# The second layer norm of a two-layer decoder trunk, re-divided between VectorE and ScalarE with GpSimd left out

## The chip, the cores and the metric

One core of a Trainium2 chip runs the whole kernel in one launch. The metric is the device time of one execution, in microseconds (us). The engines are called by the profile's short names: PE is TensorE, DVE is VectorE, ACT is ScalarE, POOL is GpSimd, SP is SyncE; SP only issues transfers here. Each engine takes its instructions strictly in the order in which the program put them on that engine's queue.

## What is computed

The program is a decoder trunk of two layers over 512 positions of 1024 features. Each layer mixes the positions, adds the residual and normalises (the first norm), then runs a mixture of experts, adds the residual and normalises again (the second norm). The second norm is what is changed:

```python
DN_ALPHA = (2.0 * DEPTH) ** 0.25
LN_EPS = 1e-5

def layer_norm(x, g, b):
    xf = x.astype(F32)
    mu = jnp.mean(xf, axis=-1, keepdims=True)
    var = jnp.mean(jnp.square(xf - mu), axis=-1, keepdims=True)
    return ((xf - mu) * lax.rsqrt(var + LN_EPS) * g.astype(F32) + b.astype(F32)).astype(x.dtype)

for layer in range(DEPTH):
    ...
    x = layer_norm(DN_ALPHA * x + mix.astype(x.dtype), ln1_g[layer], ln1_b[layer])
    ffn = hier_moe(x, ...)
    x = layer_norm(DN_ALPHA * x + ffn, ln2_g[layer], ln2_b[layer])
return x
```

## The kernel before

All products are made from float32 values split in two halves, `hi` (ACT, L195) and `lo` (DVE, L196), with three matmuls each (L200, L201, L202). The method `hilo` emits such a split; `mm3` emits the three matmuls.

The method `moe` runs the experts. Sixteen regular tiles and some overflow tiles are computed; each tile's rows are added into a DRAM tensor `yd` by a scatter that POOL issues (L1617). `yd` has been filled beforehand with the scaled residual. When the last scatter has landed, SP loads the four blocks of 128 positions back into four tiles `row`, 128 partitions by 1024 features (L1752). These are blocks 0 to 3; the second norm turns each `row` into the layer's output in place, and then `finish(tt, r)` is called.

What `finish` is differs by layer. In layer 0 it is `odd_token`: SP writes the block to the DRAM tensor `x2d` (L1291), PE transposes it in eight pieces (L209), ACT and DVE split the transposed block (L195, L196), and PE multiplies it with the value weights of the next layer's attention (24 matmuls). After block 3 PE goes on with the keys of the attention (tile `sd`), which need all four blocks. In layer 1 `finish` is one transfer to the output by SP (L1824), and block 3's transfer is the end of the program.

The norm before has these parts, each on one block `tt` or on a pair of blocks:

- `stats` (L1764): two DVE BN_STATS over 512 features (L290) and one aggregate (L1766), giving mean and variance.
- `scale` (L1770): for two blocks at once, the reciprocal root of the variance in eleven tiny DVE instructions that wait for one another (`rsqrt_steps`, L271 to L281), and a twelfth (L1773) that gives minus mean times scale.
- `norm` (L1776): the upper 512 features go through ACT (L1778), then POOL for the product with `g` (L1779), then the addition of `b`, by POOL for blocks 0 and 1 (L1781) and by DVE for blocks 2 and 3 (L1787). The lower 512 features take two DVE passes (L1782, L1784).

The generators are interleaved by `weave`, which alternates between a main generator and a side one. So the order on DVE is written out by hand: statistics of blocks 0 and 1; statistics of 2 and 3 woven with the first `scale`; norms of 0 and 1 woven with the second `scale`; norms of 2 and 3:

```python
run_all(each(stats, 0, 1))
weave(each(stats, 2, 3), scale(0))
weave(each(norm, 0, 1), scale(1))
run_all(each(norm, 2, 3))
```

`moe` calls `lnparams` for the tiles `g` and `b` (names `lng`, `lnb`) long before. The four tiles `self.xg` are the buffers of gathered rows, which no instruction reads any more by the time of the norm.

Of the kernel before, what the change touches and what calls it, by code (L numbers as in the profile page):

```python
# [8 lines left out]
F32 = mybir.dt.float32  # L9
# [4 lines left out]
AF = mybir.ActivationFunctionType  # L14
# [4 lines left out]
MUL, ADD, SUB = ALU.mult, ALU.add, ALU.subtract  # L19

L = 512
D = 1024
KD = D // 128
NT = L // 128
# [28 lines left out]
def blk(i, n=128):  # L53
    return slice(i * n, (i + 1) * n)


def weave(main, *sides):


    wait = [0] * len(sides)  # L60
    done = [False] * len(sides)

    def poke(i):
        while wait[i] <= 0 and not done[i]:
            try:
                wait[i] = next(sides[i])
            except StopIteration:
                done[i] = True
    for _ in main:
        for i in range(len(sides)):  # L70
            wait[i] -= 1
            poke(i)
    for i in range(len(sides)):
        for _ in (sides[i] if not done[i] else ()):
            pass


def run_all(gen):
    for _ in gen:
        pass  # L80
# [82 lines left out]
class Trunk:  # L163
# [99 lines left out]
        q.dma_start(bt, b.rearrange("(o d) -> o d", o=1).to_broadcast([128, D]))  # L263
        self.lnp = gt, bt

    def rsqrt_steps(self, z, var, n, pool, eps=1e-5):

        V = self.nc.vector
        t = lambda nm, dt=F32: pool.tile([128, n], dt, name="rq" + nm, bufs=4)
        h, m, y = t("h"), t("m"), t("i", I32)  # L270
        V.tensor_scalar(h, var, eps, 0.5, op0=ADD, op1=MUL)  # L271
        yield 1
        V.tensor_scalar(y, h.bitcast(I32), -0.5, float(0x5f3759df - 0x400000 - 0x80000000), op0=MUL, op1=ADD)
        y = y.bitcast(F32)
        for i in range(3):
            yield 1
            V.tensor_mul(m, y, y)
            yield 1
            V.tensor_mul(m, m, h)
            yield 1  # L280
            V.scalar_tensor_tensor(z, m, -1.5, y, op0=ADD, op1=MUL)  # L281
            y = z
# [1353 lines left out]
    def moe(self, layer, lg, between, start, before, after, finish):  # L1636
        nc, tc, mo, I = self.nc, self.tc, self.mo, self.I
# [110 lines left out]
        rows = []  # L1748
        mv = mo.tile([128, NT, 2], F32, name="bnmv4", bufs=1)
        for tt in range(NT):  # L1750
            r = mo.tile([128, D], F32, name="row", bufs=6)
# [1 line left out]
            rows.append(r)  # L1753
        after()
        V = nc.vector
        rs = mo.tile([128, NT], F32, name="lnrs", bufs=1)
        nm = mo.tile([128, NT], F32, name="lnnm", bufs=1)
        g, b = self.lnp
        lo, hi = blk(0, 512), blk(1, 512)
        sts = [mo.tile([128, 2, 6], F32, name="bnst", bufs=4) for _ in range(NT)]  # L1760

        def stats(tt):
            for h in range(2):
                self.ln_stats(sts[tt], rows[tt], h)  # L1764
                yield 1
            V.bn_aggr(mv[:, tt, :], sts[tt])  # L1766
            yield 1

        def scale(q):
            s = blk(q, 2)  # L1770
            yield from self.rsqrt_steps(rs[:, s], mv[:, s, 1], 2, mo)
            yield 1
            V.scalar_tensor_tensor(nm[:, s], mv[:, s, 0], -1.0, rs[:, s], op0=MUL, op1=MUL)  # L1773
            yield 1

        def norm(tt):  # L1776
            r = rows[tt]
            nc.scalar.activation(r[:, hi], r[:, hi], AF.Identity, scale=rs[:, tt:tt + 1], bias=nm[:, tt:tt + 1])  # L1778
            nc.gpsimd.tensor_mul(r[:, hi], r[:, hi], g[:, hi])  # L1779
            if tt < 2:  # L1780
                nc.gpsimd.tensor_add(r[:, hi], r[:, hi], b[:, hi])  # L1781
            V.scalar_tensor_tensor(r[:, lo], r[:, lo], mv[:, tt, 0:1], g[:, lo], op0=SUB, op1=MUL)  # L1782
            yield 1
            V.scalar_tensor_tensor(r[:, lo], r[:, lo], rs[:, tt:tt + 1], b[:, lo], op0=MUL, op1=ADD)  # L1784
            yield 1
            if tt >= 2:
                V.tensor_add(r[:, hi], r[:, hi], b[:, hi])  # L1787
            finish(tt, r)
            yield 1

        def each(f, *i):
            for j in i:
                yield from f(j)
        run_all(each(stats, 0, 1))
        weave(each(stats, 2, 3), scale(0))
        weave(each(norm, 0, 1), scale(1))
        run_all(each(norm, 2, 3))

    def run(self):
        nc, tc, I = self.nc, self.tc, self.I  # L1800
# [58 lines left out]
```

## Time and profile before

| what | us |
|---|---|
| median of three runs | 1006.04 |
| lowest and highest of them | 1003.46, 1008.68 |
| the profiled execution, its own time | 1003.56 |
| its span in the profile | 1001.9 |
| PE busy | 845.2 |
| DVE busy | 789.1 |
| ACT busy | 566.4 |
| POOL busy | 311.9 |

All positions in the rows below are microseconds from the start of that span; the execution's own time is 1.7 us longer. The second norm stands in the profile twice: in layer 0 from 535.97 us, when its first block has landed, and in layer 1 from 975.21 us to the end. The page's busy shares are means over the whole span and say little of these two places; they are read from the timeline of each engine in them.

### The profile page before, as it was taken

The page shows a single profiled execution, that of the slowest core. Times are in us where ns is not written, and L with a number is a line of the kernel's source. Part 1 is how long each engine was busy: PE and PEld are TensorE (multiplying, and loading weights), DVE is VectorE, ACT ScalarE, POOL GpSimd, SP SyncE. Part 2 cuts the span into 40 slices and gives each one's busy share as a digit, 9 for nine tenths or more (in the row PEclk, how much of TensorE's full clock was granted, in tenths as well). Part 3 has the DMA queues.
Part 4 walks back from the last instruction along what each step waited for, and adds up shares of the span by engine and source line. Part 5 has one row for each costly group of instructions (what it writes and reads, how often), then busy time and mean ns, then how long its engine had stood idle before and what let it go on. Part 6 is the DMA issues. An engine that isn't in the chain of part 4 may idle for free.

```text
span 1001.9 us, 13169 instructions
## 1 busy us (share of the span) xinstructions
PE 845.2 (84%) x4396; PEld 707.5 (71%) x4396; DVE 789.1 (79%) x1542; ACT 566.4 (57%) x922; POOL 311.9 (31%) x342
## 2 busy tenths in 40 slices
PE   5996999998975899999782899999993889999840
PEld 4895887787864788887661787788883668888630
DVE  6998668668679799997776657888788879999737
ACT  3331445536124899988673256656611688999721
POOL 6397971101102223222222302345611122232203
PEclk9998999999987999999995999989997799999975
DMA  9321112102947789999955350420093879999722
GB/s 280 123 93 43 43 43 95 43 1 61 358 174 260 296 299 365 371 375 305 322 177 191 105 127 1 120 50 2 4 365 140 327 251 337 361 382 362 239 65 114
DMA packets 52875, 192.05 MB, mean 192 GB/s; under 512 B 13492, under 2 KB 15552, under 8 KB 38336
## 3 DMA queue, kind: packets, MB, share of 16 engines
q1 hardware_dynamic: 37344, 156.47, 42.5%
q0 software_dynamic: 13440, 24.17, 9.2%
q10 hardware_dynamic: 2016, 10.49, 2.7%
q8 instruction: 38, 0.62, 0.2%
q14 instruction: 37, 0.30, 0.1%
HBM read 183.20 MB, written 31.98 MB: 215 GB/s over the span
## 4 chain that ended last, share of the span: by engine, by line
PE 47%; issue 15%; DVE 14%; DMA 12%; ACT 5%; POOL 5%; another core or an unknown queue 1%; ACTq 0%; SPq 0%; POOLq 0%; DVEq 0%
PE acc L200 10%; PE acc L202 10%; PE acc L201 10%; DMA yd<-row,r 8%; PE tp L209 2%; DVE u L196 2%; POOL yd L1617 2%; ACT u L195 1%; DMA xg<-x1d,r 1%; PE tp L1410 1%; POOL xg L1574 1%; DMA row<-yd 1%; PE sd L201 1%; PE sd L200 1%; POOL row L1779 1%
## 5 line engine op out<-in xcount | busy, mean ns | idle before, releaser
L200 PE MATMUL acc<-u 128*128 128x512 f32 (+1 forms) x712 | 296.5, 416 | 6.9 <-ACT u L195 6.9
L202 PE MATMUL acc<-u 128*128 128x512 f32 (+1 forms) x712 | 282.6, 397 | 5.5 <-DVE u L196 5.4
L201 PE MATMUL acc<-u 128*128 128x512 f32 (+1 forms) x712 | 281.7, 396 | 3.4 <-POOL u L196 1.9
L196 DVE TENSOR_TENSOR u<-u 128x1024 fp32r<-128x1024 f32 x142 | 172.2, 1241 | 27.0 <-ACT u L195 25.9
L195 ACT CAST u<-u 128x1024 fp32r<-128x1024 f32 x150 | 152.9, 1051 | 41.4 <-PE acc L202 36.6
L196 DVE TENSOR_TENSOR u<-rx,u 128x1024 fp32r<-128x1024 f32 x128 | 152.3, 1220 | 28.9 <-ACT u L195 27.8
L202 PEld LDWEIGHTS acc<-u 128*128 128x128 f32 x712 | 141.5, 199 | 35.6 <-DVE u L196 8.4
L200 PEld LDWEIGHTS acc<-u 128*128 128x128 f32 x712 | 143.8, 202 | 29.9 <-ACT u L195 8.7
L201 PEld LDWEIGHTS acc<-u 128*128 128x128 f32 x712 | 142.7, 200 | 25.8 <-DVE u L196 3.4
L1617 POOL DMA_INDIRECT yd<-row,r x37 | 58.8, 1588 | 239.1 <-ACT row L1616 186.8
L195 ACT CAST u<-rx 128x1024 fp32r<-128x1024 f32 x128 | 129.3, 1049 | 3.0 <-issue 1.8
L195 ACT CAST u<-tp 128x512 fp32r<-128x512 f32 x102 | 60.4, 608 | 72.0 <-PE tp L209 68.1
L196 DVE TENSOR_TENSOR u<-tp,u 128x512 fp32r<-128x512 f32 x102 | 67.8, 698 | 16.7 <-ACT u L195 16.6
L1574 POOL DMA_INDIRECT xg<-x1d,r x41 | 46.6, 1137 | 76.3 <-PE tp L209 66.2
L209 PE MATMUL tp<-idf,xg 128*128 128x128 f32 x312 | 49.9, 301 | 16.0 <-DMA xg<-x1d,r 9.8
L1400 POOL TENSOR_SCALAR P<-P,st 128x256 f32<-128x256 f32 (+3 forms) x32 | 35.1, 1097 | 90.3 <-DVE st L1376 55.2
L209 PEld LDWEIGHTS tp<-idf,xg 128*128 128x128 f32 x312 | 47.2, 208 | 21.3 <-issue 10.1
L200 PE MATMUL acc<-u,ht 128*128 128x512 f32 x148 | 58.5, 395 | 4.0 <-ACT ht L195 4.0
L202 PE MATMUL acc<-u,ht 128*128 128x512 f32 x148 | 57.7, 390 | 0.0
L201 PE MATMUL acc<-u,ht 128*128 128x512 f32 x148 | 57.6, 389 | 0.0
L1616 ACT ACTIVATE row<-acc,r 128x512 f32<-128x512 f32 x74 | 47.8, 687 | 10.0 <-PE acc L202 10.0
L1118 ACT COPY u<-tp 128x512 f32<-128x512 f32 x16 | 9.4, 587 | 66.3 <-PE tp L1117 56.3
(394 smaller groups left out, 1439.4 us busy)
## 6 DMA issues: line engine op xcount, KB each, us to landing
rx<-in_moe_w_gate_up_dram SPq DMA_DIRECT2D x48, 1024.0 KB, 10.8
u<-in_moe_w_gate_up_dram SPq DMA_DIRECT2D x24, 1024.0 KB, 16.2
u<-in_moe_w_down_dram SPq DMA_DIRECT2D x19, 1024.0 KB, 14.9
rx<-in_moe_w_down_dram SPq DMA_DIRECT2D x16, 1024.0 KB, 11.9
u<-in_ev_w_in_dram SPq DMA_DIRECT2D x10, 1024.0 KB, 6.2
u<-in_ev_w_out_dram SPq DMA_DIRECT2D x4, 1024.0 KB, 5.1
x1d<-row POOLq DMA_DIRECT2D x8, 512.0 KB, 5.6
yd<-row ACTq DMA_DIRECT2D x8, 512.0 KB, 3.6
```

The costliest lines, as they stand in the source:

```text
L195: self.nc.scalar.copy(hi, src)
L196: (self.nc.gpsimd if pool else self.nc.vector).tensor_sub(lo, src, hi)
L200: nc.tensor.matmul(ps, ah, bh, start=start, stop=False)
L201: nc.tensor.matmul(ps, ah, bl, start=False, stop=False)
L202: nc.tensor.matmul(ps, al, bh, start=False, stop=stop)
L209: self.nc.tensor.transpose(tp[:, blk(j)], src[:, s], self.idf)
L1400: nc.gpsimd.tensor_scalar(P[:, 1, :W], P[:, 1, :W], st[:, 5, 1:2], None, op0=MUL)
L1410: nc.tensor.transpose(tp[:, blk(2 * b + x)], P[:, x, blk(b0 + b)], self.idf)
L1574: nc.gpsimd.indirect_dma_start(out=xg, out_offset=None, in_=self.x1d, in_offset=bass.IndirectOffsetOnAxis(ap=self.toki[:, s:s + 1], axis=0 ...
L1616: nc.scalar.activation(ys[:, blk(c, 512)], yp[c], AF.Copy, scale=self.gate[:, s:s + 1])
L1617: return lambda: self.scattered(s, nc.gpsimd.indirect_dma_start(out=self.yd, out_offset=bass.IndirectOffsetOnAxis(ap=self.toki[:, s:s + 1] ...
L1779: nc.gpsimd.tensor_mul(r[:, hi], r[:, hi], g[:, hi])
```

## The change

It does six things.

1. POOL gets no work in the second norm. Both halves of a block are normalised by DVE at full width, in two passes of 128 by 1024: (row minus mean) times `g`, then times the scale plus `b`.
2. The statistics of blocks 2 and 3 move from DVE to ACT: one full pass `sums` gives the sum of a row, one pass `squares` gives the sum of the squared differences from the mean. Both use ACT's accumulator output; their full-size output goes into `xg` and is read by nobody. A DVE instruction `means` lies between them.
3. `rsqrt_steps` can take a sum of squares and divide by 1024 itself.
4. The twelfth instruction of `scale` (minus mean times scale) is gone.
5. In layer 0 the blocks come one by one: block 0 gets statistics, scale and norm before block 1's statistics.
6. In layer 1 blocks 0 and 1 keep a common `scale`; block 1 is normalised in halves, with the eleven instructions of the scale of blocks 2 and 3 put in threes between its four passes.

The diff, whole:

```diff
--- before.py
+++ after.py
@@ -263,12 +263,15 @@
         q.dma_start(bt, b.rearrange("(o d) -> o d", o=1).to_broadcast([128, D]))
         self.lnp = gt, bt
 
-    def rsqrt_steps(self, z, var, n, pool, eps=1e-5):
+    def rsqrt_steps(self, z, var, n, pool, eps=1e-5, of=1):
 
         V = self.nc.vector
         t = lambda nm, dt=F32: pool.tile([128, n], dt, name="rq" + nm, bufs=4)
         h, m, y = t("h"), t("m"), t("i", I32)
-        V.tensor_scalar(h, var, eps, 0.5, op0=ADD, op1=MUL)
+        if of == 1:
+            V.tensor_scalar(h, var, eps, 0.5, op0=ADD, op1=MUL)
+        else:
+            V.tensor_scalar(h, var, 0.5 / of, 0.5 * eps, op0=MUL, op1=ADD)
         yield 1
         V.tensor_scalar(y, h.bitcast(I32), -0.5, float(0x5f3759df - 0x400000 - 0x80000000), op0=MUL, op1=ADD)
         y = y.bitcast(F32)
@@ -1753,48 +1756,86 @@
             rows.append(r)
         after()
         V = nc.vector
-        rs = mo.tile([128, NT], F32, name="lnrs", bufs=1)
-        nm = mo.tile([128, NT], F32, name="lnnm", bufs=1)
         g, b = self.lnp
-        lo, hi = blk(0, 512), blk(1, 512)
-        sts = [mo.tile([128, 2, 6], F32, name="bnst", bufs=4) for _ in range(NT)]
+        t = lambda nm: mo.tile([128, NT], F32, name=nm, bufs=1)
+        rs, sm, ss = t("lnrs"), t("lnsm"), t("lnss")
+        nm = t("lnnm")
 
         def stats(tt):
+            s = mo.tile([128, 2, 6], F32, name="bnst", bufs=4)
             for h in range(2):
-                self.ln_stats(sts[tt], rows[tt], h)
-                yield 1
-            V.bn_aggr(mv[:, tt, :], sts[tt])
-            yield 1
-
-        def scale(q):
-            s = blk(q, 2)
-            yield from self.rsqrt_steps(rs[:, s], mv[:, s, 1], 2, mo)
-            yield 1
-            V.scalar_tensor_tensor(nm[:, s], mv[:, s, 0], -1.0, rs[:, s], op0=MUL, op1=MUL)
-            yield 1
+                self.ln_stats(s, rows[tt], h)
+            V.bn_aggr(mv[:, tt, :], s)
+            return mv[:, tt, 0:1], SUB
+
+
+        def sums(tt):
+            nc.scalar.activation(self.xg[tt - 2], rows[tt], AF.Identity, accum_out=sm[:, tt:tt + 1])
+
+        def means():
+            V.tensor_scalar(nm[:, 2:4], sm[:, 2:4], -1.0 / D, None, op0=MUL)
+
+        def squares(tt):
+            nc.scalar.activation(self.xg[tt - 2], rows[tt], AF.Square, bias=nm[:, tt:tt + 1], accum_out=ss[:, tt:tt + 1])
+
+        def scale(a, z):
+            s = slice(a, z)
+            if a < 2:
+                yield from self.rsqrt_steps(rs[:, s], mv[:, s, 1], z - a, mo)
+            else:
+                yield from self.rsqrt_steps(rs[:, s], ss[:, s], z - a, mo, of=D)
 
         def norm(tt):
             r = rows[tt]
-            nc.scalar.activation(r[:, hi], r[:, hi], AF.Identity, scale=rs[:, tt:tt + 1], bias=nm[:, tt:tt + 1])
-            nc.gpsimd.tensor_mul(r[:, hi], r[:, hi], g[:, hi])
-            if tt < 2:
-                nc.gpsimd.tensor_add(r[:, hi], r[:, hi], b[:, hi])
-            V.scalar_tensor_tensor(r[:, lo], r[:, lo], mv[:, tt, 0:1], g[:, lo], op0=SUB, op1=MUL)
+            m, op = (mv[:, tt, 0:1], SUB) if tt < 2 else (nm[:, tt:tt + 1], ADD)
+            V.scalar_tensor_tensor(r, r, m, g, op0=op, op1=MUL)
+            V.scalar_tensor_tensor(r, r, rs[:, tt:tt + 1], b, op0=MUL, op1=ADD)
+
+        def norm_half(tt, h):
+            r = rows[tt][:, blk(h, 512)]
+            V.scalar_tensor_tensor(r, r, mv[:, tt, 0:1], g[:, blk(h, 512)], op0=SUB, op1=MUL)
             yield 1
-            V.scalar_tensor_tensor(r[:, lo], r[:, lo], rs[:, tt:tt + 1], b[:, lo], op0=MUL, op1=ADD)
+            V.scalar_tensor_tensor(r, r, rs[:, tt:tt + 1], b[:, blk(h, 512)], op0=MUL, op1=ADD)
             yield 1
-            if tt >= 2:
-                V.tensor_add(r[:, hi], r[:, hi], b[:, hi])
-            finish(tt, r)
-            yield 1
-
-        def each(f, *i):
-            for j in i:
-                yield from f(j)
-        run_all(each(stats, 0, 1))
-        weave(each(stats, 2, 3), scale(0))
-        weave(each(norm, 0, 1), scale(1))
-        run_all(each(norm, 2, 3))
+        if layer == 0:
+            stats(0)
+            run_all(scale(0, 1))
+            norm(0)
+            stats(1)
+            finish(0, rows[0])
+            sums(2)
+            sums(3)
+            run_all(scale(1, 2))
+            means()
+            norm(1)
+            squares(2)
+            squares(3)
+            run_all(scale(2, 4))
+            finish(1, rows[1])
+            for tt in (2, 3):
+                norm(tt)
+                finish(tt, rows[tt])
+        else:
+            sums(2)
+            sums(3)
+            stats(0)
+            stats(1)
+            run_all(scale(0, 2))
+            means()
+            squares(2)
+            squares(3)
+            norm(0)
+            finish(0, rows[0])
+            z = scale(2, 4)
+            for h in range(2):
+                for _ in norm_half(1, h):
+                    for _ in range(3):
+                        next(z, None)
+            finish(1, rows[1])
+            run_all(z)
+            for tt in (2, 3):
+                norm(tt)
+                finish(tt, rows[tt])
 
     def run(self):
         nc, tc, I = self.nc, self.tc, self.I
```

The order of the instructions, with the new line numbers. In layer 0 on ACT, from the last splits of the overflow code to the value tiles of the attention (`tp` is a transposed block, `lnnm` minus the mean, `lnrs` the scale). Before:

```order
L1616 ACTIVATE row<-acc,r_2836 128x512 x2
L1746 UNCONDITIONAL_BRANCH x2
L195 CAST u<-u 128x1024 x4
L1778 ACTIVATE row<-row,lnnm,lnrs 128x512
L195 CAST u<-tp 128x4x128 x2
...
L195 CAST VH<-acc 128x256 x4
```

Now, the same stretch of ACT in layer 0:

```order
L195 CAST u<-u 128x1024 x4
L195 CAST u<-tp 128x4x128 x2
L1773 ACTIVATE xg_2424,lnsm<-row 128x1024
L1773 ACTIVATE xg_2425,lnsm<-row 128x1024
L1779 ACTIVATE xg_2424,lnss<-row,lnnm 128x1024
L1779 ACTIVATE xg_2425,lnss<-row,lnnm 128x1024
L195 CAST u<-tp 128x4x128 x6
L195 CAST VH<-acc 128x256 x4
```

Before, each block's two splits had one norm pass ahead of them; the pair of rows stands four times. Now block 0's splits come first, then the four full passes, then the splits of the other three blocks.

In layer 0 on DVE, from block 1's scale to block 3's norm:

```order
L196 TENSOR_TENSOR u<-tp,u 128x4x128 x2
L272 TENSOR_SCALAR rqh<-bnmv_5243 128x1
...
L1776 TENSOR_SCALAR lnnm<-lnsm 128x2
L1791 SCALAR_TENSOR_TENSOR row<-row,bnmv_5243,lng 128x1024
L1792 SCALAR_TENSOR_TENSOR row<-row,lnrs,lnb 128x1024
L274 TENSOR_SCALAR rqh<-lnss 128x2
...
L196 TENSOR_TENSOR u<-tp,u 128x4x128 x2
L1791 SCALAR_TENSOR_TENSOR row<-row,lnnm,lng 128x1024
L1792 SCALAR_TENSOR_TENSOR row<-row,lnrs,lnb 128x1024
```

Block 0's splits now stand in front of block 1's scale, `means` and the scale of blocks 2 and 3 stand around block 1's norm, and block 1's splits wait behind that scale.

In layer 1 on DVE, from `means` to the middle of block 1:

```order
L1776 TENSOR_SCALAR lnnm<-lnsm 128x2
L1791 SCALAR_TENSOR_TENSOR row<-row,bnmv_10018,lng 128x1024
L1792 SCALAR_TENSOR_TENSOR row<-row,lnrs,lnb 128x1024
L1796 SCALAR_TENSOR_TENSOR row<-row,bnmv_10018,lng 128x512
L274 TENSOR_SCALAR rqh<-lnss 128x2
L276 TENSOR_SCALAR rqi<-rqh 128x2
L280 TENSOR_TENSOR rqm<-rqi 128x2
L1798 SCALAR_TENSOR_TENSOR row<-row,lnrs,lnb 128x512
```

`means`, which waits for ACT's `sums`, now stands ahead of block 0's norm, and the tiny instructions of the last scale stand between the half-width passes of block 1.

## Rows read from the trace of the kernel before

**Rows 1.** Tail by engine: stretch, PE, PEld, DVE, ACT, POOL, clock, DMA share, GB/s

```profile
975.20:998.20 23.00, 0.00 (x0) 0.00 (x0) 20.73 (x46) 3.04 (x4) 9.20 (x6) 0.50 0.32 125
```

**Rows 2.** Chain of waits, 950 to 1002: start us, us, what

```profile
972.83 5.71 DMA row<-yd
...
983.88 1.71 POOL row L1779
...
988.69 1.71 POOL row L1781
...
992.76 1.62 POOL row L1779
```

**Rows 3.** Timeline of DVE, tail of layer 1: start, us, engine, line, operation

```profile
975.21 1.29 DVE L290 BATCH_NORM_STATS2 bnst<-row 128x6 f32<-128x512 f32 x2 [11.66 <-DMA row<-yd]
...
982.34 0.16 DVE L279 TENSOR_TENSOR rqm<-rqm,rqh 128x2 f32<-128x2 f32 x1
982.54 0.16 DVE L281 SCALAR_TENSOR_TENSOR lnrs<-rqm,lnrs 128x2 f32<-128x2 f32 x1
...
982.93 0.75 DVE L1782 SCALAR_TENSOR_TENSOR row<-row,bnmv,lng 128x512 f32<-128x512 f32 x1
...
984.39 1.23 DVE L273 TENSOR_SCALAR rqi<-rqh 128x2 int32<-128x2 int32 x1
...
985.83 1.66 DVE L1782 SCALAR_TENSOR_TENSOR row<-row,bnmv,lng 128x512 f32<-128x512 f32 x1
...
989.21 1.21 DVE L281 SCALAR_TENSOR_TENSOR lnrs<-rqm,rqi 128x2 f32<-128x2 f32 x1
...
994.41 1.73 DVE L1787 TENSOR_TENSOR row<-row,lnb 128x512 f32<-128x512 f32 x1 [1.16 <-POOL row L1779]
...
997.51 0.68 DVE L1787 TENSOR_TENSOR row<-row,lnb 128x512 f32<-128x512 f32 x1
```

**Rows 4.** Timeline, layer 0: the first block and the last, all engines

```profile
535.97 1.29 DVE L290 BATCH_NORM_STATS2 bnst<-row 128x6 f32<-128x512 f32 x2 [1.79 <-DMA row<-yd]
...
545.50 1.09 PE L209 MATMUL tp<-idf,row 128*128 128x128 f32 x4 [18.53 <-DVE row L1784]
...
546.68 0.59 ACT L195 CAST u<-tp 128x512 fp32r<-128x512 f32 x1 [1.93 <-PE tp L209]
...
547.30 0.69 DVE L196 TENSOR_TENSOR u<-tp,u 128x512 fp32r<-128x512 f32 x1 [0.75 <-ACT u L195]
...
565.12 0.68 DVE L1787 TENSOR_TENSOR row<-row,lnb 128x512 f32<-128x512 f32 x1
...
570.38 0.40 PE L200 MATMUL sd<-u 128*128 128x512 f32 x1
```

**Rows 5.** Groups of instructions, shapes apart: count, busy us, mean ns

```profile
L293 DVE SCALAR_TENSOR_TENSOR row<-row,bnmv,lng 128x1024 f32<-128x1024 f32 x8 | 10.2, 1275 | 0.0
...
L1129 ACT ACTIVATE row<-row 128x1024 f32<-128x1024 f32 x8 | 8.5, 1060 | 1.6 <-ACT row L1129 1.2 <-DMA xg<-x1d,r 0.4
...
L1386 ACT ACTIVATION_READ_ACCUMULATOR P<-acc,st 128x1 f32 x64 | 12.9, 202 | 0.0
```

**Rows 6.** Loads of blocks 2 and 3 in layer 1 (L1752): issue, time to landing

```profile
L1752 SPq DMA_DIRECT2D row<-yd x2: 376/379/382, 972.8 to 973.3; - x2
...
DMA to landing us min/median/max: 5.7/6.1/6.5
```

**Rows 7.** Chain of waits in layer 0: single matmuls at the two clocks

```profile
562.15 0.21 PE acc L200
...
565.57 0.12 PE acc L201
```

**Rows 8.** Busy time as in Rows 1, two stretches of layer 0

```profile
562.00:563.00 1.00, 1.00 (x6) 1.00 (x6) 0.84 (x2) 0.83 (x2) 0.09 (x1) 0.50 0.78 311
...
565.00:566.00 1.00, 1.00 (x11) 1.00 (x11) 0.80 (x2) 0.00 (x0) 0.00 (x0) 1.00 0.00 0
```

## The prediction

> **What bounds the kernel at the two places.** I read the tail of layer 1 first, because nothing comes after it. The busy time by engine [rows 1] says that from 975.2 to 998.2 us DVE is busy 20.73 of 23.00 us, POOL 9.20 and ACT 3.04, and that PE does nothing. So this stretch is DVE work with a second engine beside it. The chain of waits [rows 2] shows which of the two ends last: behind the landing of the blocks come four POOL steps of 1.6 to 1.7 us, a fifth left out, so POOL's half of each block sets the end and DVE waits for it. The timeline of DVE [rows 3] shows the second price. A tiny instruction takes 0.16 us by itself, and 1.23 and 1.21 us at 984.39 and 989.21; a half-width pass takes 0.75 us by itself and 1.66 us at 985.83; an addition takes 0.68 us by itself and 1.73 us at 994.41. The long ones all lie beside a POOL product or addition. Those four rows hold 1.07 + 1.05 + 0.91 + 1.05 = 4.1 us that DVE spent on nothing.
>
> The row alone says that DVE runs slower beside POOL. The Trainium skill (SBUF — State Buffer, Who interferes with whom) explains it: the two share one pair of ports, and the one that comes second is blocked until the other's instruction is done. The trace agrees, with 1.2 us for an instruction of 0.16 us; by the rule a kernel without POOL work here would give back those 4.1 us and no more on DVE, against the 4.6 us that the step-by-step sum below gives.
>
> In layer 0 the same norm feeds PE. From the first landing at 535.97 to the last addition, which ends at 565.12 + 0.68 = 565.80 us, lie 29.8 us, and PE starts the keys at 570.38 us [rows 4]. The distance from the last row of block 3 to the keys, 4.6 us, is eight transposes, a split and 24 matmuls.
>
> **Prices.** A full-width DVE pass: 1.275 us [rows 5]; with 0.04 us to the next dependent one, two passes are 2.6 us. One link of the eleven-step scale: 0.20 us, from 982.34 to 982.54 [rows 3], so 2.15 us for a scale that nothing interrupts. Statistics of one block on DVE: 1.29 us [rows 3] plus about 0.2 for the aggregate, 1.5 us. A full-width ACT pass with an accumulator does not occur before. The nearest row is ACT's 128 by 1024 pass at 1.060 us, and the accumulator's read-out is 0.202 us [rows 5]; the pass lies between 1.06 (read-out hidden) and 1.26 us (not hidden). I take 1.2, and all of it counts where something waits. Splits of block pieces on ACT and DVE: 0.59 and 0.69 us; four transposes 1.09 us at the low clock [rows 4].
>
> **Layer 1, step by step.** Blocks 0 and 1 have landed as before; block 2 lands at 972.8 + 5.7 = 978.5 and block 3 at 973.3 + 6.5 = 979.8 us [rows 6].
> - ACT, idle here before, starts `sums` of block 2 at 978.6; `sums` of block 3 ends at 981.05.
> - DVE: two statistics from 975.2 to 978.15, scale to 980.3. `means` waits for ACT until 981.1, a new wait of 0.8 us, and the whole rest of the norm stands behind it in DVE's queue. Done 981.3.
> - Block 0's two passes: 983.9. `squares` of blocks 2 and 3 run beside them on ACT, 981.4 to 983.9, so they cost nothing; were they later, the first tiny instruction of the last scale, second in line after block 0, would wait.
> - Block 1: four half passes at about 0.7 and eleven tiny instructions at about 0.2, a few of them hidden by a half pass: 4.5 us, to 988.4. Not hidden at all they would make 4.9.
> - Blocks 2 and 3: 2 x 2.6 = 5.2, to 993.6 us.
>
> Before, the last addition ended at 997.51 + 0.68 = 998.2 [rows 3], and the span ran another 3.7 us for the output transfer. The last two transfers leave 2.6 us apart, and I take it that the last finds its queue free as before, so I keep 3.7: the end is 997.3 against 1001.9. **Gain 4.6 us.** With the ACT price at its ends (1.06 or 1.26), `means` moves by 0.3 or 0.1 us.
>
> **Layer 0, step by step.**
> - Block 0: statistics, scale and two passes from 535.97 make 1.5 + 2.15 + 2.6, to 542.3. PE starts 3.1 us earlier than its 545.50.
> - Block 0's eight transposes at the low clock take 2.2 us; its splits end on ACT at 545.2 and on DVE at 545.9. DVE does block 1's statistics under them, then waits some 0.7 us in all.
> - ACT then does `sums` of blocks 2 and 3 to 547.8, covered by DVE's scale of block 1, 545.9 to 548.1. `means` 548.3, block 1's passes 550.9; `squares` on ACT 548.4 to 550.9, covered by them.
> - The scale of blocks 2 and 3, 551.0 to 553.1. Block 1's splits wait behind it and end at 554.5.
> - Block 2's passes 557.1; its transposes and splits hold DVE until 559.9, of which 1.3 us is waiting.
> - Block 3's passes: 562.6 us, against 565.8. With the 4.6 us that follow, the keys start at 567.2 instead of 570.4.
>
> I take 2.9 of these 3.2 us, for the few waits between engines that I left out. What comes after the keys is unchanged and waits for PE, ACT and DVE work, not for these loads, so I let the gain reach the end. **Gain 2.9 us.**
>
> The smaller edits cost nothing of their own: the twelfth instruction of a scale (0.16 us, twice) is in the sums; the output of ACT's passes goes to tiles nobody reads; SP's transfers of `x2d` stay in the same order on its queue and follow the blocks.
>
> **Sum.** 4.6 + 2.9 = 7.5 us off the profiled execution's 1003.56 gives 996.1 us. That execution lies 2.5 us under the median of the runs, 1006.04, near their lowest. What is measured is a median, so I set 1006.04 - 7.5 = 998.5 us.
>
> **Rivals.**
> - *PE falls to its low clock in layer 0.* Its granted clock there goes between the two levels already: 0.50 (1.2 GHz) at 562 and 1.00 (2.4 GHz) at 565 [rows 8], after a stretch in which PE waited for block 2's rows; a step between matmuls is 0.21 us at one and 0.12 us at the other [rows 7]. With the change block 0's matmuls end by 544.5 + 24 x 0.21 = 549.6, block 1 comes at 550.9, and its `lo` products wait until 553.8. If the low clock then holds through block 3, its transposes cost 1.0 us more and its matmuls 22 x 0.09 = 2.0 more, and layer 0 gives nothing: 4.6 us in all, 1001.4. Against it: from 553.8 on PE has work in most of the time, and in the rows too the clock is up again for block 3. If every block from 1 on and the first keys ran low, layer 0 would lose 3.2 us, and the sum would be a gain of 1.4, 1004.6: the worst end. The Trainium skill (TensorE: Matmul & The Clock Gate, Part 1: The HAM clock gate) says that the gate follows how busy the array has lately been; by that rule the longer gaps speak against this change, and the time would be the 1001.4 of this rival. The rows agree as far as the clock falls after a gap here too. Chance 0.20.
> - *Full-width DVE passes are slowed by what runs beside them.* This is the slower end. All of both norms now hangs on DVE: 8 blocks with two passes each, 16 in full widths. Before, a pass beside POOL took 1.66 instead of 0.75, 2.2 times as long. If ACT's passes on neighbouring tiles or the transfers did the same, a pass would be 2.8 us and the kernel 16 x 1.5 - 7.5 = 16.5 us slower, 1022; it turns from a gain to a loss at 7.5 / 16 = 0.47 us more per pass, 1.75 us. Against it: the 1.275 us were measured in the first norm, with ACT and transfers at work. Chance 0.05.
> - *The tail alone gains,* because what layer 0 wins is lost at a later wait: 4.6 us, 1001.4. Chance 0.06; the steps behind the keys show no wait for a load.
>
> That the change does not do what it says is excluded by the order of the instructions.
>
> **How the numbers follow.** About 0.5% (5.0 us, 1001.0) is what a measurement of this kernel can tell from no change. My forecast has 0.69. Its gain of 7.5 could be 5 to 9.5, and a median of a few runs that spread over 5 us is uncertain by some 2 us, so 0.60 of it is faster by more than 0.5%. The rivals at 1001.4 add 0.06 there and 0.20 within 0.5%. Faster 0.66, same 0.29, slower 0.05. The range runs from 994.0 (9.5 us off, and a low median) to 1003.5 (the first rival with some more, and a high median).
>
> **What would show it.** In the profile afterwards: DVE in the tail without a single tiny instruction over 0.3 us; `means` about 0.8 us late behind ACT; the last DVE pass ending near 993.6 minus what layer 0 gave, that is some 18.4 us after the first landing instead of 23.0; full-width passes at 1.28 and ACT passes at 1.06 us; in layer 0 the keys 31.2 to 31.5 us after the first landing instead of 34.4. I am wrong if ACT's passes are above 1.3 us, if the granted clock is 0.50 at block 3's matmuls, or if the distance from the keys to the tail's first landing has grown by more than a microsecond.

## The result and the profile after

The changed kernel took 995.94 us (median of four runs, 994.25 to 998.43); the kernel before, beside it, 1006.9 us (four runs, 1003.46 to 1008.68). The ratio is 0.9897, 95% interval 0.9862 to 0.9932. A second comparison on one chip (run e0_again below) gave 0.9904 (0.9882 to 0.9926). The profiled execution took 996.19 us, with a span of 994.4 us.

The busy time of the whole page: POOL's part of the norm is gone (311.9 us before, 292.6 now), and the other engines' sums hardly moved:

```profile
PE 847.0 (85%) x4396; PEld 708.4 (71%) x4396; DVE 785.0 (79%) x1537; ACT 569.6 (57%) x930; POOL 292.6 (29%) x330
```

The two places show where the gain comes from. I measure two stretches in every profile: the **norm of layer 0**, from the start of the first DVE statistic to the first matmul of the keys, and the **tail**, from the first statistic of layer 1 to the end of the span.

| profile | norm of layer 0 | from the keys to the tail | tail |
|---|---|---|---|
| before | 34.41 | 404.83 | 26.69 |
| after | 30.16 | 403.22 | 22.72 |
| difference | -4.25 | -1.61 | -3.97 |

Together the two stretches are 8.2 us shorter. The long stretch between them has no changed instruction; over the twelve profiles of this study it lies between 402.6 and 406.4 us and goes with no edit, so its 1.6 us are scatter. The same holds ahead of the norm of layer 0: its first statistic begins at 538.30 us here and at 535.97 before, and over the twelve profiles between 534.5 and 538.5. So the two spans differ by 7.5 us and the two stretches by 8.2.

DVE in the tail, from the timeline of the changed kernel:

```profile
971.68 1.29 DVE L293 BATCH_NORM_STATS2 bnst<-row 128x6 f32<-128x512 f32 x2 [11.73 <-DMA row<-yd]
...
976.61 0.16 DVE L284 SCALAR_TENSOR_TENSOR lnrs<-rqm,lnrs 128x2 f32<-128x2 f32 x1
978.18 0.17 DVE L1776 TENSOR_SCALAR lnnm<-lnsm 128x2 f32<-128x2 f32 x1 [1.41 <-ACT xg L1773]
978.31 1.29 DVE L1791 SCALAR_TENSOR_TENSOR row<-row,bnmv,lng 128x1024 f32<-128x1024 f32 x1
979.63 1.29 DVE L1792 SCALAR_TENSOR_TENSOR row<-row,lnrs,lnb 128x1024 f32<-128x1024 f32 x1
980.83 0.75 DVE L1796 SCALAR_TENSOR_TENSOR row<-row,bnmv,lng 128x512 f32<-128x512 f32 x1
981.49 0.16 DVE L274 TENSOR_SCALAR rqh<-lnss 128x2 f32<-128x2 f32 x1
...
985.15 1.28 DVE L1791 SCALAR_TENSOR_TENSOR row<-row,lnnm,lng 128x1024 f32<-128x1024 f32 x1
...
988.99 1.28 DVE L1792 SCALAR_TENSOR_TENSOR row<-row,lnrs,lnb 128x1024 f32<-128x1024 f32 x1
```

Against [rows 3]: no tiny instruction of a scale is longer than 0.17 us, no half pass longer than 0.75, and the last pass ends 18.59 us after the first landing (988.99 + 1.28 - 971.68) instead of 23.0. The new wait stands in brackets: 1.41 us for ACT's sums.

ACT in the tail, same timeline:

```profile
975.72 1.06 ACT L1773 ACTIVATE xg<-row 128x1024 f32<-128x1024 f32 x1 [15.31 <-DMA row<-yd]
976.69 0.19 ACT L1773 ACTIVATION_READ_ACCUMULATOR xg<-row 128x1 f32 x1
977.00 1.06 ACT L1773 ACTIVATE xg<-row 128x1024 f32<-128x1024 f32 x1
...
978.38 1.15 ACT L1779 ACTIVATE xg<-row,lnnm 128x1024 f32<-128x1024 f32 x1 [0.23 <-DVE lnnm L1776]
979.44 0.19 ACT L1779 ACTIVATION_READ_ACCUMULATOR xg<-row,lnnm 128x1 f32 x1
979.53 1.13 ACT L1779 ACTIVATE xg<-row,lnnm 128x1024 f32<-128x1024 f32 x1
```

A full pass that sums is 1.06 us, one that squares 1.13 to 1.15 us; the read-out of 0.19 us begins 0.1 us before its pass ends, so a pass is ready 1.15 to 1.25 us after its start.

In layer 0, DVE at the first statistic, at the end of block 1's passes and at the last two blocks, timeline of the changed kernel:

```profile
538.30 1.29 DVE L293 BATCH_NORM_STATS2 bnst<-row 128x6 f32<-128x512 f32 x2 [1.83 <-DMA row<-yd]
...
551.25 1.28 DVE L1792 SCALAR_TENSOR_TENSOR row<-row,lnrs,lnb 128x1024 f32<-128x1024 f32 x1
...
557.03 1.28 DVE L1792 SCALAR_TENSOR_TENSOR row<-row,lnrs,lnb 128x1024 f32<-128x1024 f32 x1
559.75 1.29 DVE L196 TENSOR_TENSOR u<-tp,u 128x512 fp32r<-128x512 f32 x2 [1.43 <-ACT u L195]
560.95 1.27 DVE L1791 SCALAR_TENSOR_TENSOR row<-row,lnnm,lng 128x1024 f32<-128x1024 f32 x1
562.26 1.28 DVE L1792 SCALAR_TENSOR_TENSOR row<-row,lnrs,lnb 128x1024 f32<-128x1024 f32 x1
```

And PE there, the transposes of blocks 1 and 3 and the first matmul of the keys:

```profile
552.68 1.06 PE L209 MATMUL tp<-idf,row 128*128 128x128 f32 x8 [1.09 <-DVE rqh L274]
...
563.69 1.06 PE L209 MATMUL tp<-idf,row 128*128 128x128 f32 x8 [0.32 <-DVE row L1792]
...
568.46 0.40 PE L200 MATMUL sd<-u 128*128 128x512 f32 x1
```

Block 3 is ready at 563.54 and PE's transposes follow it at once; from there to the keys it is 4.9 us, against 4.6 [rows 4]. PE's granted clock is 1.00 from 551 us on, where before it fell to 0.50 again at 562 [rows 8].

### The profile page after: what moved, and what is told of

It is laid out like the page before. It is cut to its first block, busy times and chain, and to the rows that moved or that the text cites. A ratio compares the mean times of both kernels' runs of the same rounds, so it can differ in the third digit from the quotient of the medians.

```text
span 994.4 us, 13138 instructions
## 1 busy us (share of the span) xinstructions
PE 847.0 (85%) x4396; PEld 708.4 (71%) x4396; DVE 785.0 (79%) x1537; ACT 569.6 (57%) x930; POOL 292.6 (29%) x330
## 4 chain that ended last, share of the span: by engine, by line
PE 41%; DVE 23%; issue 14%; DMA 13%; ACT 5%; POOL 3%; another core or an unknown queue 1%; SPq 1%; ACTq 1%; POOLq 0%; DVEq 0%
PE acc L200 8%; PE acc L202 8%; PE acc L201 8%; DMA yd<-row,r 8%; DVE u L196 5%; PE tp L209 3%; POOL yd L1620 2%; ACT u L195 2%; PE tp L1413 1%; PE sd L201 1%; POOL xg L1577 1%; DMA row<-yd 1%; PE sd L202 1%; PE sd L200 1%; PE sd L1137 1%
```

## The experiments

Ratios are against the kernel before; e0 to e3 share one group of its runs, e4 to e7 a second (without e6_second_look), and e8 has a third.

| run | ratio, 95% interval | norm of layer 0 | tail |
|---|---|---|---|
| e0_again | 0.9904 (0.9882 to 0.9926) | 30.17 | 22.67 |
| e1_layer1_new | 0.9952 (0.9934 to 0.9970) | 34.55 | 22.27 |
| e2_layer0_new | 0.9962 (0.9948 to 0.9976) | 30.15 | 26.26 |
| e3_stats_dve | 0.9957 (0.9938 to 0.9975) | 34.66 | 23.98 |
| e4_pool_beside | 1.0001 (0.9987 to 1.0015) | 33.59 | 27.06 |
| e5_layer0_pairs | 0.9935 (0.9911 to 0.9960) | 31.43 | 22.58 |
| e6_center_first | 0.9900 (0.9881 to 0.9920) | 30.15 | 22.85 |
| e6_second_look | one execution, no ratio | 30.15 | 21.82 |
| e7_last_in_halves | 0.9899 (0.9878 to 0.9921) | 30.13 | 21.54 |
| e8_fill_both | 0.9885 (0.9867 to 0.9903) | 29.67 | 21.09 |

### Again, and the two places apart: e0_again, e1_layer1_new, e2_layer0_new

e0_again is the changed kernel without an edit. The other two keep the old norm beside the new and choose by layer:

```diff
+        if layer == 0:                      # e1; in e2 the other way round
+            run_all(each(ostats, 0, 1))
+            weave(each(ostats, 2, 3), oscale(0))
+            weave(each(onorm, 0, 1), oscale(1))
+            run_all(each(onorm, 2, 3))
+        else:
+            ...
```

> The changed kernel itself, once more beside the kernel before on one chip. From the two profiles the norm of layer 0 (first landing to the first matmul of the keys) went from 34.4 to 30.2 us and the tail (first landing to the end) from 26.7 to 22.7, together 8.2 us, or 0.992 of the kernel before. Theory (all of the gain lies in these two stretches): 0.992, and the two stretches again at 30.2 and 22.7 us. Rival (some 2 us more are won elsewhere): 0.990 or less again.

> The new norm in layer 1 alone, layer 0 as before. Theory (the two places are separate and add up): the tail takes 22.7 us and the norm of layer 0 34.4, the gain is 4.0 us, 0.996. Rival (the tail alone carries the gain, or what layer 0 wins is lost later): the whole 8 to 10 us, 0.990 to 0.992.

> The new norm in layer 0 alone, layer 1 as before. Theory: layer 0 takes 30.2 us, the tail 26.7, the gain is 4.2 us, 0.996, and the stretch from the keys to the tail is as long as before within its own scatter of 1 to 2 us. Rival (layer 0's gain is lost at a later wait): within 1 us of the kernel before, 0.999 to 1.000, with that stretch some 4 us longer.

Measured: e0_again 994.6 us against 1004.25. Its stretches are 30.17 and 22.67 us, both as in the first profile to 0.05 us. The 0.992 that the 8.2 us make of 1004 lies inside both intervals, so no gain from elsewhere is needed; but 0.9904 lies nearer to the rival's 0.990, and the median alone, 9.6 us, is too coarse to exclude a microsecond or two. The layer-1 kernel has the tail of the new kernel (22.27) and the norm of the old (34.55), and 0.9952, 4.8 us; the layer-0 kernel has 30.15 and 26.26, and 0.9962, 3.8 us. The two gains add to 8.6 us. The tail does not carry the gain alone, and what layer 0 wins is not lost later: from its keys to its tail it is 405.2 us, 0.3 more than before.

### The statistics back on DVE: e3_stats_dve

```diff
-            sums(2)
-            sums(3)
             run_all(scale(1, 2))
-            means()
+            stats(2)
+            stats(3)
             norm(1)
-            squares(2)
-            squares(3)
```

and the same in layer 1; the last scale reads the variance of BN_STATS.

> The changed kernel with the statistics of blocks 2 and 3 back on DVE, so ACT's four full passes and the wait for them are gone. Theory (DVE's queue sets the end in both places): two statistics more, 3.0 us, less the instruction for the means (0.2 us) and, in the tail, less the 1.4 us that DVE waited for ACT there: layer 0 33.0 us and the tail 24.1 us, together 4.2 us slower than the changed kernel, 0.996 of the kernel before. Rival (moving the statistics to ACT was worth nothing, the new wait took it back): both stretches within 0.5 us of 30.2 and 22.7.

Measured: 0.9957, that is 4.3 us. Of the 9.6 us that the changed kernel gains in this group 5.3 are given back; by the stretches it is 4.5 in layer 0 and 1.3 in the tail, 5.8 together. The tail is as expected, 23.98 us. The norm of layer 0 is 34.66 instead of 33.0: 1.7 us more than DVE's extra work. Block 1 is ready 2.8 us later (16.99 us after the first landing, 14.23 in the changed kernel), which is that extra work. The granted clock accounts for the rest, in this kernel's busy time by stretch (columns as in [rows 1]):

```profile
550.00:554.00 4.00, 0.00 (x0) 0.00 (x0) 3.93 (x6) 0.00 (x0) 0.00 (x0) 1.00 0.00 0
556.00:562.00 6.00, 5.55 (x26) 5.25 (x26) 3.84 (x5) 0.03 (x1) 0.00 (x0) 0.50 0.26 104
```

PE does nothing for four microseconds before block 1 comes, and its clock then stands at 0.50 (1.2 GHz) while block 1 is multiplied. DVE waits for block 2's transposes behind those matmuls. Block 1's last pass and that wait, in the timeline of the same kernel:

```profile
552.83 1.28 DVE L1788 SCALAR_TENSOR_TENSOR row<-row,lnrs,lnb 128x1024 f32<-128x1024 f32 x1
...
563.07 1.29 DVE L196 TENSOR_TENSOR u<-tp,u 128x512 fp32r<-128x512 f32 x2 [3.20 <-ACT u L195]
```

3.20 us where the changed kernel waits 1.43: the 1.8 us. So ACT's passes take some 2.8 us of work off DVE in layer 0 (4.5 less 1.7), and they also keep PE at work early enough to hold its clock. This is the first rival of the prediction, seen in another kernel. It is seen in one execution, of 1004.01 us where the median is 1000.24; that the clock falls so in all of them is not shown.

Against the kernel before, this run shows what the change gives without the statistics on ACT. In its profile the tail is 2.7 us shorter (23.98 against 26.69) and the norm of layer 0 no shorter (34.66 against 34.41, the 1.7 us of PE's clock included). The ratio gives 4.3 us, 2.5 to 6.2 by its interval, where the two stretches give 2.5; so how much layer 0 gains without the statistics on ACT in other executions stays open.

### POOL work that nobody needs: e4_pool_beside

```diff
+            nc.gpsimd.tensor_mul(self.xg[2][:, 0:512], rows[3][:, 0:512], g[:, 0:512])
+            for _ in range(5):
+                nc.gpsimd.tensor_mul(self.xg[2][:, 0:512], self.xg[2][:, 0:512], g[:, 0:512])
```

> The changed kernel with six half-width POOL products on a tile that nobody reads, started by the landing of block 3 in each second norm; no engine needs their result. Theory (a POOL product holds up the DVE instruction beside it): tiny DVE instructions of 1.2 us and half passes of 1.7 us appear again, and each stretch grows by 4 to 6 us: layer 0 34 to 36 us, the tail 27 to 29 us. Rival (POOL cost time before only because DVE and the transfers waited for its results): no DVE instruction is longer, both stretches within 0.5 us of 30.2 and 22.7.

Measured: 1.0001 against the kernel before, the whole gain gone, with six POOL products in each norm that no engine waits for. The tail of this kernel on POOL and DVE:

```profile
982.15 1.26 POOL L1801 TENSOR_TENSOR xg<-row,lng 128x512 f32<-128x512 f32 x1 [15.05 <-DMA row<-yd]
983.49 9.33 POOL L1803 TENSOR_TENSOR xg<-xg,lng 128x512 f32<-128x512 f32 x5
...
984.72 2.17 DVE L1792 SCALAR_TENSOR_TENSOR row<-row,lnrs,lnb 128x1024 f32<-128x1024 f32 x1
986.82 1.75 DVE L1796 SCALAR_TENSOR_TENSOR row<-row,bnmv,lng 128x512 f32<-128x512 f32 x1
988.49 1.22 DVE L274 TENSOR_SCALAR rqh<-lnss 128x2 f32<-128x2 f32 x1
989.74 0.17 DVE L276 TENSOR_SCALAR rqi<-rqh 128x2 int32<-128x2 int32 x1
989.94 1.10 DVE L280 TENSOR_TENSOR rqm<-rqi 128x2 f32<-128x2 f32 x1
...
991.63 1.21 DVE L282 TENSOR_TENSOR rqm<-rqm,rqh 128x2 f32<-128x2 f32 x1
992.88 0.16 DVE L284 SCALAR_TENSOR_TENSOR lnrs<-rqm,rqi 128x2 f32<-128x2 f32 x1
```

The long instructions are back while POOL runs, and gone when it ends at 992.82. Five of them hold 0.9 + 1.0 + 1.1 + 0.9 + 1.1 = 5.0 us more than they take in the changed kernel; the tail grew by 4.3 us, as expected. The norm of layer 0 grew by 3.4, less than the 4 to 6 expected: three instructions of block 1's scale were held there, for 1.0 us each. The first of them, in DVE's timeline:

```profile
548.63 1.14 DVE L284 SCALAR_TENSOR_TENSOR lnrs<-rqm,rqi 128x1 f32<-128x1 f32 x1
```

The two sides hold up each other: a POOL product takes 1.26 us while DVE waits (982.15), and the five that follow take 9.33 us here, 1.87 us each, and 6.73 us in layer 0. The tail of the kernel before had five long instructions too. [rows 3] show four of them, 4.1 us, and this is the fifth, so that DVE lost 5.1 us there:

```profile
987.41 1.21 DVE L279 TENSOR_TENSOR rqm<-rqm,rqh 128x2 f32<-128x2 f32 x1
```

That POOL cost time only through the results it delivered is excluded; that DVE's delay beside it is real is shown. Which part of the old cost was which is not told apart by this run, since the products do not lie where the old ones lay.

### Layer 0 in pairs: e5_layer0_pairs

```diff
-        if layer == 0:
-            stats(0)
-            ...
-        else:
-            sums(2)
+        sums(2)
+        ...
```

> The changed kernel with layer 0 in the order of layer 1 (blocks 0 and 1 share a scale), so block by block is undone and nothing else. Theory (an early block 0 gives PE, ACT and DVE the transposes and splits while DVE goes on): the keys start 2.5 us later, layer 0 32.7 us, tail 22.7. Rival (DVE has the same work in any order, so only its sum counts): layer 0 within 0.5 us of 30.2.

Measured: 31.43 us, halfway between the two. Against the order of layer 1, its halves of block 1 included, the block-by-block order is worth 1.3 us, half of what I worked out. The timelines of DVE show two sides of it. Up to block 3's passes DVE waits 5.3 us in this norm and 1.9 us in the changed kernel; but a common scale for blocks 0 and 1 saves it a scale of 2.1 us. The two longest waits that the changed kernel does not have, in this kernel's timeline:

```profile
543.38 0.17 DVE L1776 TENSOR_SCALAR lnnm<-lnsm 128x2 f32<-128x2 f32 x1 [1.37 <-ACT xg L1773]
...
548.00 0.69 DVE L196 TENSOR_TENSOR u<-tp,u 128x512 fp32r<-128x512 f32 x1 [1.89 <-ACT u L195]
```

In the changed kernel's layer 0 no DVE instruction waits for ACT's `sums`, and the wait for block 0's splits is 0.49 us.

### Filling the new wait: e6_center_first, e6_second_look, e7_last_in_halves

```diff
             run_all(scale(0, 2))
+            center(0)                       # block 0's first pass
             means()
             squares(2)
             squares(3)
-            norm(0)
+            spread(0)                       # block 0's second pass
```

> The changed kernel with one edit in layer 1: block 0's first pass, which needs no result of ACT, stands ahead of the means instead of behind them. Theory (the 1.4 us that DVE waits there for ACT's sums is idle time on the path): the pass of 1.3 us fills it, the tail takes 21.4 us. Rival (the squares start later by what the means are late, and the last scale then waits for them): the tail stays within 0.3 us of 22.7.

> As the run before, and the last block of layer 1 is normalised and written out in halves of 512 features, the second half by ACT's queue. Theory (the last transfer of 512 KB stands alone at the end, half of it can go 1.3 us earlier): the tail another 0.6 us shorter, 20.8 us. Rival (the four half passes and the second transfer cost what the shorter transfer gives): within 0.2 us of the run before.

> The kernel with block 0's first pass ahead of the means, one look more. In its first profile block 1 landed 0.9 us later than block 0's statistics ended, so that DVE reached the means late and the squares were late too. Theory: where block 1 lands in time, the first tiny instruction of the last scale starts some 8.9 us after the first landing instead of 9.8, and the last DVE pass ends 17.7 us after it. Rival (the edit is worth nothing however the blocks land): 18.5 us or more.

e7 also has:

```diff
+            for h in range(2):
+                r = rows[3][:, blk(h, 512)]
+                ...
+                (nc.scalar if h else nc.sync).dma_start(self.out[0, blk(3), blk(h, 512)], r)
```

Measured: the first profile of e6 shows no gain in the tail (22.85), the second 21.82, where 21.4 was expected. Their DVE timelines differ in one landing. First profile:

```profile
971.90 1.29 DVE L293 BATCH_NORM_STATS2 bnst<-row 128x6 f32<-128x512 f32 x2 [0.92 <-DMA row<-yd]
...
979.44 0.17 DVE L274 TENSOR_SCALAR rqh<-lnss 128x2 f32<-128x2 f32 x1 [0.54 <-ACT xg L1779]
```

Second profile:

```profile
973.52 1.23 DVE L293 BATCH_NORM_STATS2 bnst<-row 128x6 f32<-128x512 f32 x2
...
981.01 0.17 DVE L274 TENSOR_SCALAR rqh<-lnss 128x2 f32<-128x2 f32 x1 [0.54 <-ACT xg L1779]
...
988.51 1.28 DVE L1795 SCALAR_TENSOR_TENSOR row<-row,lnrs,lnb 128x1024 f32<-128x1024 f32 x1
```

In the first, block 1 landed 0.92 us too late for DVE, so the means came late and there was no wait to fill; in the second they came in time, and the last scale starts 8.9 us after the first landing (972.08) instead of 9.8, with the last DVE pass ending 17.71 us after it, as expected. In both the rival takes back a part: 0.54 us of waiting for the squares. So the edit is worth 0.8 to 0.9 us where the blocks land in time. Where block 1 is late it is worth nothing, and the profile of e0_again, the changed kernel without an edit, shows why. Block 1 is 0.80 us late there too, and the wait for ACT's sums takes up the delay, 0.41 us instead of 1.41:

```profile
970.46 1.29 DVE L293 BATCH_NORM_STATS2 bnst<-row 128x6 f32<-128x512 f32 x2 [0.80 <-DMA row<-yd]
...
974.57 0.17 DVE L1776 TENSOR_SCALAR lnnm<-lnsm 128x2 f32<-128x2 f32 x1 [0.41 <-ACT xg L1773]
```

The last DVE pass ends 18.52 us after the first landing there, and 18.77 in e6's first profile. The last pass of e7, in its timeline:

```profile
989.50 0.75 DVE L1849 SCALAR_TENSOR_TENSOR row<-row,lnrs,lnb 128x512 f32<-128x512 f32 x1
```

e7 ends 3.45 us after this pass, and 4.11 us in e6's second profile: the second half's shorter transfer gives 0.7 us, and the four half passes take back 0.4. The tail is 21.54 us, 0.3 shorter than in e6's second profile, where 0.6 was expected. On the ratios alone e6, e7 and the changed kernel cannot be told apart.

### A version with the waits filled: e8_fill_both

```diff
-            for h in range(2):
-                for _ in norm_half(1, h):
-                    for _ in range(3):
-                        next(z, None)
+            halves = [norm_half(1, h) for h in range(2)]
+            for n, k in zip(halves + halves, (0, 4, 4, 4)):
+                next(n)
+                for _ in range(k):
+                    next(z, None)
```

```diff
-            for tt in (2, 3):
-                norm(tt)
-                finish(tt, rows[tt])
+            norm(2)
+            center(3)
+            finish(2, rows[2])
+            spread(3)
+            finish(3, rows[3])
```

> The run with the last block in halves, and two edits more. In layer 1 both first half passes of block 1 stand ahead of the last scale, so that DVE does not wait for ACT's squares; in layer 0 the first pass of block 3 stands ahead of block 2's splits, in the 1.4 us that DVE waits for them. Theory: the 0.5 us wait for the squares in the tail goes, 21.0 us if the blocks land as in that run (21.5); in layer 0 block 3 is ready 1.3 us earlier, but PE is still at block 2's matmuls until 0.3 us before its transposes, so only 0.3 us are won, 29.8 us. Rival (DVE alone sets the pace in layer 0): 28.9 us.

Measured: 992.93 us against 1003.53, 0.9885 (0.9867 to 0.9903), the lowest ratio of all, though its interval still overlaps the changed kernel's. The tail is 21.09 us, and the wait for the squares is gone, in the timeline of this kernel:

```profile
980.39 0.16 DVE L274 TENSOR_SCALAR rqh<-lnss 128x2 f32<-128x2 f32 x1
```

In layer 0 the result is 29.67 us, as PE allows and not as DVE would. DVE at the last two blocks, same timeline:

```profile
561.17 1.28 DVE L1795 SCALAR_TENSOR_TENSOR row<-row,lnrs,lnb 128x1024 f32<-128x1024 f32 x1
564.71 1.29 DVE L196 TENSOR_TENSOR u<-tp,u 128x512 fp32r<-128x512 f32 x2 [2.26 <-ACT u L195]
```

and PE's transposes of block 3 there:

```profile
563.45 1.04 PE L209 MATMUL tp<-idf,row 128*128 128x128 f32 x8
```

Block 3 is ready at 562.45, and PE begins its transposes a microsecond later with no wait of its own: it was at block 2's matmuls. Here PE has become the bound of the last two blocks.

## Why the prediction was right

- **What bounded the tail.** POOL's chain and DVE's delay beside POOL were read as the cost; the tail lost 3.97 us of a worked-out 4.6. The delay is shown by e4 (POOL work alone brings the time back); by e3 2.7 us of the gain come without the statistics on ACT and 1.3 with them. That POOL's chain set the old end is read from [rows 2] and was not tried by itself. The rule of the Trainium skill (SBUF — State Buffer, Who interferes with whom) that GpSimd and VectorE hold each other up agrees: e4 is its case, with no result of POOL used by anyone. The 4.1 us that the prediction set beside this rule count four long instructions of five; they were no term of the sum.
- **The steps of the tail.** The first scale ended 5.1 us after the first landing, as worked out. The new wait for ACT was 1.41 us where I had 0.8, because `sums` began 4.0 us after the first landing (975.72) and not 3.4: blocks 2 and 3 landed a little later against block 0 than in the profile before. Block 1 in halves took 4.3 us (4.5 worked out), the ACT passes 1.06 to 1.15. The last pass came at 18.59 us (18.4). The end came 4.1 us after it, where I kept 3.7. Nine of the other profiles end a full-size transfer, four of them, e1 with the same tail code among them, 3.7 us after the last pass and five 4.1; in e1 (3.7) and e3 (4.1) the transfer lands 2.6 us after its issue alike, so the 0.4 us lie behind the landing, and no row shows their cause.
- **The steps of layer 0.** The order of events was as worked out, the size was not: 4.25 us instead of 2.9. This is the term that was mis-sized. The lead over the sums grew from block to block: block 0's norm ended 6.2 us after the landing (6.3), block 1's passes 14.2 (14.9), block 2's 20.0 (21.1), block 3's 25.2 (26.6), 1.4 us early. Of these, 0.3 were lost again on the way from block 3 to the keys (4.9 us for 4.6). I had also taken 0.3 us off for waits left out, and did not need them: 2.9 + 1.4 - 0.3 + 0.3 = 4.3. A likely source of the 1.4 us, not tried by itself: a DVE instruction that does not need the one before it starts about 0.1 us before that one ends, and there are some ten of these (last section).
- **The sum.** 7.5 us worked out, 8.2 us in the two stretches. That the sum is nearer than its terms is luck: the tail gave 0.6 us less than worked out and layer 0 1.4 more. The medians differ by 11.0 in the first comparison and 9.6 in the second, where single runs of one kernel spread over 4 to 7.5 us; the 1 to 3 us beyond 8.2 are not explained by any row and lie inside the intervals.
- **The rivals.** PE's low clock did not come back after block 0 in the changed kernel: between blocks 0 and 1 PE was idle for 1.1 us there, against four in e3, where the clock was 0.50 afterwards. The rule of the Trainium skill (TensorE: Matmul & The Clock Gate, Part 1: The HAM clock gate) that the clock follows what the engine did before agrees with e3 and does not bite in the changed kernel. That rival's time would have been 1001.4. Full-width passes were not slowed by ACT or by transfers: 1.285 us beside both, 1.275 us [rows 5] before. What layer 0 won was not lost later (e2).

## What to carry to other kernels

A second engine is no help if it slows the first: before dividing elementwise work between DVE and POOL, look for DVE instructions of one shape with two durations, the long one beside a POOL instruction. The difference, less the time that POOL's work takes on DVE, is what moving that work back can give; here, in the profile of e3, it gave 2.7 us in the tail and nothing in layer 0. Where statistics can go to an engine that is idle anyway, put work that does not need them ahead of the instruction that waits for them, and see what then waits next. In a chain of blocks through several engines, giving PE its next block earlier can also keep its clock up, as e3 shows from the other side.

## What was not expected

Instructions on DVE that do not depend on each other overlap a little. In the changed kernel's layer 0 a pass of 1.28 us that starts at 543.23 is followed by the next block's statistics, which do not need it, at 544.43, 1.20 us later; a pass that needs the one before it starts 1.31 us after (555.72, then 557.03). With some ten such hand-overs between independent instructions in the norm of layer 0 this makes about a microsecond, as much as layer 0 gained beyond its steps (4.25 against 3.2). The count is a reading of the timeline. And the landing of four loads that are issued together scatters between profiles: in two of the twelve block 1 reached the tail 0.8 to 0.9 us too late for DVE. That is enough to hide an edit worth as much: the first profile of e6_center_first alone would have said that it does nothing.
